# The activations' buffers moved off the weight buffers' place modulo 512 bytes

## The chip, the cores and the metric

The kernel runs on one core of a Trainium2 chip. The metric is the device time of one execution in microseconds (us). A core has a matrix engine (TensorE, PE in the profile; its weight loads are listed as PEld), a vector engine (VectorE, DVE), a scalar engine (ScalarE, ACT), GpSimd (POOL) and a queue that issues DMAs (SyncE, SP). They work side by side and wait for each other through semaphores. On-chip memory (SBUF) has 128 partitions; a tile occupies the same byte range in each of them, so "place" and "distance" below are byte addresses within a partition. Matmul results go to another memory, PSUM.

## The reference

One decoder layer on 256 tokens of width 2048, in float32: a norm, one wide projection `w_in`, three branches that are gated and summed, an output projection, and a squared-ReLU MLP, each with a residual, and a last norm.

```python
proj = rms_norm(x, norm_mix_g) @ w_in                   # 2048 x 11264
u_s5, u_lru, q, k, v, gate_logits = split(proj)
merged = (g_s5 * (s5(u_s5) @ w_br_s5) + g_lru * (rglru(u_lru) @ w_br_lru)
          + g_attn * (stick_breaking(q, k, v) @ w_br_attn))
h = x + merged @ w_out
h = h + square(relu(rms_norm(h, norm_mlp_g) @ w_up)) @ w_down   # hidden width 8192
return rms_norm(h, final_norm_g)
```

The S5 and RG-LRU branches are scans over the tokens, the third is an attention over 8 heads. Inside the S5 branch stands one more weight matrix, `w_glu`.

## The kernel before

All large matrix products run in pieces of one size. A weight **unit** is 256 rows by 512 columns of a weight matrix (two groups of 128 rows); the list `stream` has 520 of them, in the order in which they are used. A unit is loaded by DMA into a `raw` tile (`load_next`, L130) and split into two tiles of a reduced-precision type (`split_next`): ScalarE writes the high part `hi` (L146), VectorE the low part `lo` = raw - hi (L147). The activations are split in the same way into a high and a low part. A product is then the sum of three matmuls, high x high, high x low and low x high.

A matmul has a stationary operand of 128 x 128, which a separate instruction (a weight load, LDWEIGHTS, on PEld) brings into the engine, and a moving operand of 256 or 512 columns that streams past it. The load for the next matmul is issued while the current one streams. There are two kinds of product:

- `chunk` (matmuls at L225 to L227) has the weights stationary and 256 columns of activations moving. It serves `w_in` for the branches' inputs u, k and q, and `w_glu`: 72 units, 24 matmuls each.
- `chunk_tok` (L241 to L243) and `pair_tok` (L276 to L278) have the activations stationary and 512 columns of weights moving. They serve all other units, 12 matmuls each. In the very last chunk eight units do half of their work in pieces of 256 columns.

Smaller matmuls stand in between: those of the S5 scan (`ps_v` at L665 from the tile `stk`, `ps_y` at L653), of attention (`ps_z`, `ps_c`, `ps_o` from `kT`, `tri`, `vt`), of the RG-LRU gates and of the norms. Their work is spread over the stream by generators that `pump` advances after every unit. The order of the matmuls on PE is that of the program.

The tiles come from pools that lie one behind another in SBUF, each tile on a multiple of 32 bytes. The pools up to `tmp` are, in this order:

| pool | tiles | bytes of one | place modulo 512 |
|---|---|---|---|
| `const` | par, ones, tri and others | small | ones, tri: 160 |
| `wraw` | raw x 3 | 4096 | 32 |
| `whi` | hi x 4, lo x 4 | 4096 | 32 |
| `act` | m16 (xT, merged, hT), xhi (xhi, hhi), xlo (xlo, hlo) | 16384 | 32 |
| `ypool` | yhi x 2, ylo x 2 | 8192 | 32 |
| `tmp` | gate x 3, gbias | 2048 | 32 |

The slices of a tile that a matmul reads start at multiples of 512 bytes, so two slices have the distance of their tiles modulo 512. Behind `tmp` lies the pool `s5`, whose small tiles `rad` (128 bytes) and `fw` (256 bytes) bring what follows them to 416 modulo 512: `stk` (which shares its buffer with `wrwi`), the tiles of the RG-LRU branch, and `kT`, `qT`, `vt`, `z` and `s` of attention. These are 384 bytes away from the weight buffers modulo 512, `tri` 128 bytes.

The tags `yhi` and `ylo` hold, one after another, the high and low parts of the RG-LRU branch (`ylru_hi`, `ylru_lo`), two scratch tiles of the S5 scan, the parts of the attention's output, of the gated S5 output and of the merged branches, and the MLP's hidden values (`hd_hi`, `hd_lo`).

Of the kernel before, what the change touches and what calls it, by code (L numbers as in the profile page):

```python
# [9 lines left out]
F32 = mybir.dt.float32  # L10
F32R = mybir.dt.float32r
# [3 lines left out]
P = 128  # L15
L = 256
D = 2048
KT = D // P
# [3 lines left out]
WT = W // P  # L22
NG = 64
NT = 4
# [22 lines left out]
def hybrid_block(ctx: ExitStack, tc: tile.TileContext, io, out):  # L47
# [5 lines left out]
    whi = ctx.enter_context(tc.tile_pool(name="whi", bufs=4))  # L53
    act = ctx.enter_context(tc.tile_pool(name="act", bufs=1))
    ypool = ctx.enter_context(tc.tile_pool(name="ypool", bufs=2))
    tmp = ctx.enter_context(tc.tile_pool(name="tmp", bufs=2))
    psm = ctx.enter_context(tc.tile_pool(name="psm", bufs=4, space=PSUM))
    pss = ctx.enter_context(tc.tile_pool(name="pss", bufs=4, space=PSUM))
# [234 lines left out]

    tc.keep_in_program_order(nc.scalar.preload_act_table_set("natural_log_exp_and_others"))
    gm = small("norm_mix_g")
    xT = act.tile([P, KT, L], F32, tag="m16", name="xT")
    xhi = act.tile([P, KT, L], F32R, tag="xhi", name="xhi")
    xlo = act.tile([P, KT, L], F32R, tag="xlo", name="xlo")
    load_x(0)
    for q in range(3):  # L300
        load_next()
# [212 lines left out]
        yield  # L514
        yield from lru_load()

    ylru_hi = ypool.tile([P, WT, L], F32R, tag="yhi", name="ylru_hi")
    ylru_lo = ypool.tile([P, WT, L], F32R, tag="ylo", name="ylru_lo")

    def lru_half(c, us):  # L520
        parts = []
# [111 lines left out]
    gq = []  # L633

    def s5_scan():
        v = ypool.tile([P, 2, NT, L], F32, tag="yhi", name="s5_v")
        t12 = ypool.tile([P, 2, NT, L], F32, tag="ylo", name="s5_t")
        vr, vi, t1, t2 = v[:, 0], v[:, 1], t12[:, 0], t12[:, 1]
        tabs, more = s5_tables(0)
        yield from more  # L640
        s5_split(0)
        yield
        yield
        for t in range(NT):
            s5_stack(t)
            yield
        tt = nc.vector.tensor_tensor

        def out_products(b):
            ps = pss.tile([P, CH], F32, tag="ps", name=f"ps_y{b}")  # L650
            for k, w_ in enumerate((t2, t1)):
                for t in range(NT):
                    nc.tensor.matmul(ps[t * 32:t * 32 + 32, 0:L], ce[:, k, b * NT + t, :, :], w_[:, t, :], start=k == 0, stop=k == 1,  # L653
                                     skip_group_check=True, tile_position=(0, t * 32))
            nc.vector.scalar_tensor_tensor(us5[:, b, :], us5[:, b, :], dsk[:, b:b + 1], ps[:, 0:L], ALU.mult, ALU.add)
            if b % 2:
                gq.append(later([gelu(b)], 1.0))

        for b in range(WT):
            c, s = tabs  # L660
            t3 = pp.tile([P, NT, L], F32, tag="t3", name=f"t3_{b}")
            for t in range(NT):
                ps = pss.tile([P, CH], F32, tag="ps", name=f"ps_v{b}")
                for i in range(2):
                    nc.tensor.matmul(ps[:, i * L:(i + 1) * L], stk[:, t, 1, i * P:(i + 1) * P], stk[:, t, 0, :], start=i == 0, stop=True,  # L665
                                     skip_group_check=True)
                nc.scalar.copy(v[:, :, t, :], v2(ps))
                if t % 2:
                    yield
            more = iter(())  # L670
            if b + 1 < WT:
                s5_split(b + 1)
                tabs, more = s5_tables(b + 1)
                yield
            next(more, None)
            if b:
                out_products(b - 1)
            yield
            tt(t1, vr, c, ALU.mult)
            yield  # L680
            tt(t2, vi, s, ALU.mult)
            yield
            tt(t1, t1, t2, ALU.add)
            yield
            tt(t3, vi, c, ALU.mult)
            yield
            tt(vr, vr, s, ALU.mult)
            yield
            tt(t3, t3, vr, ALU.subtract)
            next(more, None)  # L690
            yield
            for x_ in (t1, t3):
                for t in range(NT):
                    j = b * NT + t
                    tt_scan(x_[:, t, :], rad[:, j:j + 1].broadcast_to([P, L]), x_[:, t, :])
                    if b + 1 < WT and x_ is t1:
                        s5_stack(t)
                    yield
            next(more, None)
            tt(t2, t1, c, ALU.mult)  # L700
            yield
            tt(vr, t3, s, ALU.mult)
            next(more, None)
            yield
            tt(t2, t2, vr, ALU.subtract)
            yield
            tt(vi, t3, c, ALU.mult)
            yield
            tt(t1, t1, s, ALU.mult)
            yield  # L710
            tt(t1, t1, vi, ALU.add)
            yield
        for _ in range(3):
            yield
        out_products(WT - 1)
# [26 lines left out]
            if n % step == step - 1:  # L742
                yield

    merged = act.tile([P, KT, L], F32, tag="m16", name="merged")
    m_tok = merged.rearrange("p k l -> p (k l)").rearrange("p (t c) -> p t c", t=2)

    def gates(idx, c, alloc):
# [39 lines left out]

    at = ExitStack()
    ap_ = at.enter_context(tc.tile_pool(name="attn", bufs=1))  # L790
    ya_hi = ypool.tile([P, WT, L], F32R, tag="yhi", name="ya_hi")
    ya_lo = ypool.tile([P, WT, L], F32R, tag="ylo", name="ya_lo")
    Z = 384

    def diag(t):
# [84 lines left out]
        finish(t)  # L880


    yg_hi = ypool.tile([P, WT, L], F32R, tag="yhi", name="yg_hi")
    yg_lo = ypool.tile([P, WT, L], F32R, tag="ylo", name="yg_lo")
    for q in range(4):
        s = slice(2 * q, 2 * q + 2)
        nc.scalar.activation(yg_hi[:, s, :], us5[:, s, :], AF.Copy, scale=0.5)
        nc.vector.scalar_tensor_tensor(yg_lo[:, s, :], us5[:, s, :], 0.5, yg_hi[:, s, :].bitcast(F32), ALU.mult, ALU.subtract)
    ys_hi = ypool.tile([P, WT, L], F32R, tag="yhi", name="ys_hi")
    ys_lo = ypool.tile([P, WT, L], F32R, tag="ylo", name="ys_lo")  # L890
    for c in range(2):
        banks = chunk("w_glu", c, W, lambda kt: (yg_hi[:, kt, :], yg_lo[:, kt, :]))
        for j in range(2):
# [10 lines left out]

    def split_pair(i, n, src):
        if mg[i // 8] is None:
            mg[i // 8] = tuple(ypool.tile([P, WT, L], F32R, tag=t, name=f"mg_{t}{i}") for t in ("yhi", "ylo"))
        h_, l_ = mg[i // 8]
        d = slice(i % 8, i % 8 + n)
        nc.scalar.copy(h_[:, d, :], src)  # L910
        nc.vector.tensor_tensor(l_[:, d, :], src, h_[:, d, :].bitcast(F32), ALU.subtract)
# [32 lines left out]

    later([x_load()], 1.0)
    mf.append(chained(mq, split_tok(3, mlp.tile([P, 4, L], F32, tag="reluT", name="mT3", bufs=2))))
    hT = act.tile([P, KT, L], F32, tag="m16", name="hT")
    hhi = act.tile([P, KT, L], F32R, tag="xhi", name="hhi")
    hlo = act.tile([P, KT, L], F32R, tag="xlo", name="hlo")
    h_tok = mlp.tile([P, 2, D], F32, name="h_tok")  # L950

    def ms(kt):
# [114 lines left out]
    for q in range(NQ):  # L1067
        hd, hf = {}, {}

        def up_done(cu, banks):  # L1070
            c = cu % (FQ // CH)
            if c % 2 == 0:
                hd[c // 2] = (ypool.tile([P, WT, L], F32R, tag="yhi", name=f"hd_hi{q}_{c}"),
                              ypool.tile([P, WT, L], F32R, tag="ylo", name=f"hd_lo{q}_{c}"))
            h_, l_ = hd[c // 2]
            r = mlp.tile([P, 2, CH], F32, tag="relu", name=f"relu{q}_{c}", bufs=2)
            for t in range(2):
                nc.scalar.activation(r[:, t, :], banks[t], AF.Relu)
            k = slice((c % 2) * 4, (c % 2) * 4 + 4)
            hf[c] = chained(hq, hidden(r, h_[:, k, :], l_[:, k, :], f"{q}_{c}"))  # L1080

        if q == 0:
            pair_tok("w_up", 0, D, hs, up_done)
        for c in range(0 if q else 2, FQ // CH):
            up_done(c, chunk_tok("w_up", q * (FQ // CH) + c, D, hs))

        def hs_(kt):
            need(hq, hf[kt // 4])
            h_, l_ = hd[kt // 8]
            return h_[:, kt % 8, :], l_[:, kt % 8, :]  # L1090

        for task in tasks:
            finish(task)

        def down_done(c, banks):
            s = slice(c * CH, (c + 1) * CH)
            for t in range(2):
                down_evac(t, s, banks[t])
            if q == NQ - 1:
                for t in range(2):  # L1100
                    square(t, s, c)
                    if c > 0:
# [78 lines left out]
```

## Time and profile before

| | us |
|---|---|
| median of 2 runs | 1491.62 (1490.56 to 1492.67) |
| the profiled execution | 1491.41 |
| its span, first to last instruction | 1489.7 |

The busy time of an engine is the union of its instructions' times. Rows of groups give a line, engine, operation, output <- inputs (tile names without buffer numbers), size and count, then the busy time in us and the mean duration of one in ns. Matmuls are pipelined: a row of 389 ns overlaps with the next one, and the distance between starts is shorter than that. Rows of a stretch give from:to in us, the length, and for each engine the busy time with the number of its instructions that touch the stretch. Rows of the timeline begin with an instruction's start and duration in us.

### The profile page before, as it was taken

What the parts mean: (1) busy time and instruction counts of PE and PEld (TensorE: products, weight loads), DVE (VectorE), ACT (ScalarE), POOL (GpSimd) and SP (SyncE); (2) the same over time, 40 slices, a digit from 0 to 9 for tenths busy, and PEclk for the clock granted to TensorE, in tenths of its full rate; (3) what the DMA queues carried; (4) which work ended last, traced back from release to release, by engine and by line L of the source; (5) the groups of instructions that cost most, each with busy time, mean ns of one, the idle gap of its engine ahead of it and who ended that gap; (6) DMA issues with size and microseconds to landing.
All of it is one profiled execution on the core that took longest, in us unless ns stands there. A gap on an engine that the chain in (4) does not pass through costs nothing.

```text
span 1489.7 us, 19903 instructions
## 1 busy us (share of the span) xinstructions
PE 1478.5 (99%) x7518; PEld 1259.3 (85%) x7518; DVE 1175.7 (79%) x1470; ACT 775.4 (52%) x915; POOL 48.4 (3%) x73
## 2 busy tenths in 40 slices
PE   9999999999999999999999999999999999999997
PEld 9998888989888888888888888888888888888886
DVE  6878999887989998789799896568754886458955
ACT  6767556565765564544454544344433453344443
POOL 1400000000000000000000000000000000000010
PEclk9999999999999999999999999999999999999999
DMA  9557776655556756566856657666666566666664
GB/s 274 189 157 216 209 229 208 184 165 188 170 177 199 224 184 210 188 187 210 268 183 189 195 184 222 189 193 188 200 194 196 187 197 197 192 190 196 189 198 137
DMA packets 89570, 292.41 MB, mean 196 GB/s; under 512 B 12802, under 2 KB 17026, under 8 KB 89346
## 3 DMA queue, kind: packets, MB, share of 16 engines
q1 hardware_dynamic: 89042, 290.55, 62.5%
q8 instruction: 59, 0.97, 0.3%
q10 hardware_dynamic: 432, 0.59, 0.1%
q14 instruction: 37, 0.30, 0.1%
HBM read 282.71 MB, written 2.10 MB: 191 GB/s over the span
## 4 chain that ended last, share of the span: by engine, by line
PE 95%; DVE 2%; ACT 1%; DMA 1%; issue 1%; DVEq 0%; ACTq 0%; SPq 0%
PE mt_w_in L241 7%; PE mt_w_in L243 7%; PE mt_w_in L242 7%; PE mt_w_up L241 7%; PE mt_w_up L243 7%; PE mt_w_up L242 7%; PE mp_w_down L278 4%; PE mp_w_down L277 4%; PE mp_w_down L276 4%; PE mt_w_down L242 4%; PE mt_w_down L241 4%; PE mt_w_down L243 4%; PE mm_w_in L225 3%; PE mm_w_in L227 3%; PE mm_w_in L226 3%; PE mt_w_br_attn L241 1%
## 5 line engine op out<-in xcount | busy, mean ns | idle before, releaser
L146 ACT CAST hi<-raw 128x1024 fp32r<-128x1024 f32 (+1 forms) x521 | 545.2, 1050 | 614.2 <-PE mt_w_up L243 116.8
L147 DVE TENSOR_TENSOR lo<-raw,hi 128x1024 fp32r<-128x1024 f32 (+1 forms) x521 | 637.1, 1224 | 276.2 <-ACT hi L146 268.5
L241 PE MATMUL mt_w_in<-hi,xhi 128*128 128x512 f32 x448 | 176.2, 393 | 0.0
L243 PE MATMUL mt_w_in<-hi,xlo 128*128 128x512 f32 x448 | 174.5, 389 | 0.0
L242 PE MATMUL mt_w_in<-lo,xhi 128*128 128x512 f32 x448 | 174.4, 389 | 0.0
L241 PE MATMUL mt_w_up<-hi,hhi 128*128 128x512 f32 x448 | 174.3, 389 | 0.0
L242 PE MATMUL mt_w_up<-lo,hhi 128*128 128x512 f32 x448 | 174.3, 389 | 0.0
L243 PE MATMUL mt_w_up<-hi,hlo 128*128 128x512 f32 x448 | 174.3, 389 | 0.0
L225 PE MATMUL mm_w_in<-xhi,hi 128*128 128x256 f32 x512 | 146.7, 287 | 0.7 <-ACT hi L146 0.7
L227 PE MATMUL mm_w_in<-xhi,lo 128*128 128x256 f32 x512 | 145.6, 285 | 1.4 <-DVE lo L147 1.4
L226 PE MATMUL mm_w_in<-xlo,hi 128*128 128x256 f32 x512 | 145.6, 285 | 0.0
L741 DVE STREAM_TRANSPOSE reluT<-relu 32x256 f32<-32x256 f32 x256 | 111.5, 436 | 4.2
L242 PE MATMUL mt_w_down<-lo,hd_hi 128*128 128x512 f32 (+1 forms) x272 | 102.5, 377 | 0.0
L241 PE MATMUL mt_w_down<-hi,hd_hi 128*128 128x512 f32 (+1 forms) x272 | 102.4, 377 | 0.0
L243 PE MATMUL mt_w_down<-hi,hd_lo 128*128 128x512 f32 (+1 forms) x272 | 102.4, 376 | 0.0
L225 PEld LDWEIGHTS mm_w_in<-xhi,hi 128*128 128x128 f32 x512 | 99.1, 194 | 1.9 <-ACT hi L146 1.0
L227 PEld LDWEIGHTS mm_w_in<-xhi,lo 128*128 128x128 f32 x512 | 98.8, 193 | 1.9 <-DVE lo L147 1.8
L276 PE MATMUL mp_w_down<-hi,hd_hi 128*128 128x512 f32 x256 | 99.6, 389 | 0.0
L277 PE MATMUL mp_w_down<-lo,hd_hi 128*128 128x512 f32 x256 | 99.6, 389 | 0.0
L278 PE MATMUL mp_w_down<-hi,hd_lo 128*128 128x512 f32 x256 | 99.6, 389 | 0.0
L226 PEld LDWEIGHTS mm_w_in<-xlo,hi 128*128 128x128 f32 x512 | 99.2, 194 | 0.1
L243 PEld LDWEIGHTS mt_w_in<-hi,xlo 128*128 128x128 f32 x448 | 84.1, 188 | 17.7
(294 smaller groups left out, 2358.1 us busy)
## 6 DMA issues: line engine op xcount, KB each, us to landing
raw<-in_w_in SPq DMA_DIRECT2D x175, 512.0 KB, 4.2
raw<-in_w_up SPq DMA_DIRECT2D x128, 512.0 KB, 4.3
raw<-in_w_down SPq DMA_DIRECT2D x128, 512.0 KB, 4.2
raw<-in_w_out SPq DMA_DIRECT2D x32, 512.0 KB, 4.4
raw<-in_w_br_lru SPq DMA_DIRECT2D x16, 512.0 KB, 4.6
raw<-in_w_br_attn SPq DMA_DIRECT2D x16, 512.0 KB, 4.3
raw<-in_w_br_s SPq DMA_DIRECT2D x16, 512.0 KB, 4.3
stk<-ux SPq DMA_DIRECT2D x96, 64.0 KB, 4.3
```

Of the source, the lines that this page charges most:

```text
L146: anchor["act"] = nc.scalar.copy(h[:, k, :], r[:, k, :]).ins
L147: anchor["dve"] = nc.vector.tensor_tensor(l_[:, k, :], r[:, k, :], h[:, k, :].bitcast(F32), ALU.subtract).ins
L225: nc.tensor.matmul(o, wh[:, kk, s], xh, start=first and ct % 2 == 0, stop=False, skip_group_check=True)
L226: nc.tensor.matmul(o, wh[:, kk, s], xl, start=False, stop=False, skip_group_check=True)
L227: mm = nc.tensor.matmul(o, wl[:, kk, s], xh, start=False, stop=last and ct % 2 == 1, skip_group_check=True)
L241: nc.tensor.matmul(banks[j], xh[:, s], wh[:, a:b], start=kt == 0, stop=False)
L242: nc.tensor.matmul(banks[j], xh[:, s], wl[:, a:b], start=False, stop=False)
L243: return nc.tensor.matmul(banks[j], xl[:, s], wh[:, a:b], start=False, stop=kt == ng * UK - 1)
L276: nc.tensor.matmul(o, xh[:, s], wh[:, kk, :], start=kt == 0, stop=False)
L277: nc.tensor.matmul(o, xh[:, s], wl[:, kk, :], start=False, stop=False)
L278: mm = nc.tensor.matmul(o, xl[:, s], wh[:, kk, :], start=False, stop=kt == ng * UK - 1)
L741: nc.vector.transpose(d_[32 * a:32 * a + 32, :, :, 32 * b:32 * b + 32], s_[32 * b:32 * b + 32, :, :, 32 * a:32 * a + 32])
```

## The change

Every tile of the activations' high and low parts, and the tiles that share their tags, get a few unused floats at their end: 8 behind m16, 16 behind xhi, 8 behind xlo, and 24 behind each of the two yhi and two ylo buffers. A helper makes the wider tile and gives out a view of its first columns in the old shape.

```diff
+    def ytile(shape, dt, tag, name, pool=None, pad=24):
+        n = math.prod(shape[1:])
+        t = (pool or ypool).tile([P, n + pad], dt, tag=tag, name=name)[:, 0:n]
+        k = " ".join(f"d{i}" for i in range(len(shape) - 1))
+        return t.rearrange(f"p ({k}) -> p {k}", **{f"d{i}": d for i, d in enumerate(shape[1:])})
...
-    xT = act.tile([P, KT, L], F32, tag="m16", name="xT")
-    xhi = act.tile([P, KT, L], F32R, tag="xhi", name="xhi")
-    xlo = act.tile([P, KT, L], F32R, tag="xlo", name="xlo")
+    xT = ytile([P, KT, L], F32, "m16", "xT", act, 8)
+    xhi = ytile([P, KT, L], F32R, "xhi", "xhi", act, 16)
+    xlo = ytile([P, KT, L], F32R, "xlo", "xlo", act, 8)
...
-    ylru_hi = ypool.tile([P, WT, L], F32R, tag="yhi", name="ylru_hi")
-    ylru_lo = ypool.tile([P, WT, L], F32R, tag="ylo", name="ylru_lo")
+    ylru_hi = ytile([P, WT, L], F32R, tag="yhi", name="ylru_hi")
+    ylru_lo = ytile([P, WT, L], F32R, tag="ylo", name="ylru_lo")
```

The same replacement is made for every other tile of these tags (`merged`, `hT`, `hhi`, `hlo`, `s5_v`, `s5_t`, `ya_*`, `yg_*`, `ys_*`, `mg_*`, `hd_*`). The places that result, as distances from the weight buffers modulo 512, are: m16 0, xhi 32, xlo 96, the two yhi buffers 128 and 224, the two ylo buffers 320 and 416. The pads sum to 512 bytes, so that `tmp` and everything behind it keeps its place modulo 512. In the list above, `act` and `ypool` are all that moves.

More of the change, by code (lines that the diff above doesn't have):

```diff
@@ L635, in s5_scan @@
     def s5_scan():
-        v = ypool.tile([P, 2, NT, L], F32, tag="yhi", name="s5_v")
-        t12 = ypool.tile([P, 2, NT, L], F32, tag="ylo", name="s5_t")
+        v = ytile([P, 2, NT, L], F32, tag="yhi", name="s5_v")
+        t12 = ytile([P, 2, NT, L], F32, tag="ylo", name="s5_t")
         vr, vi, t1, t2 = v[:, 0], v[:, 1], t12[:, 0], t12[:, 1]
@@ L743, in blocks @@
                 yield
-    merged = act.tile([P, KT, L], F32, tag="m16", name="merged")
+    merged = ytile([P, KT, L], F32, "m16", "merged", act, 8)
     m_tok = merged.rearrange("p k l -> p (k l)").rearrange("p (t c) -> p t c", t=2)
@@ L790, in hybrid_block @@
     ap_ = at.enter_context(tc.tile_pool(name="attn", bufs=1))
-    ya_hi = ypool.tile([P, WT, L], F32R, tag="yhi", name="ya_hi")
-    ya_lo = ypool.tile([P, WT, L], F32R, tag="ylo", name="ya_lo")
+    ya_hi = ytile([P, WT, L], F32R, tag="yhi", name="ya_hi")
+    ya_lo = ytile([P, WT, L], F32R, tag="ylo", name="ya_lo")
     Z = 384
@@ L880, in hybrid_block @@
         finish(t)
-    yg_hi = ypool.tile([P, WT, L], F32R, tag="yhi", name="yg_hi")
-    yg_lo = ypool.tile([P, WT, L], F32R, tag="ylo", name="yg_lo")
+    yg_hi = ytile([P, WT, L], F32R, tag="yhi", name="yg_hi")
+    yg_lo = ytile([P, WT, L], F32R, tag="ylo", name="yg_lo")
     for q in range(4):
@@ L888, in hybrid_block @@
         nc.vector.scalar_tensor_tensor(yg_lo[:, s, :], us5[:, s, :], 0.5, yg_hi[:, s, :].bitcast(F32), ALU.mult, ALU.subtract)
-    ys_hi = ypool.tile([P, WT, L], F32R, tag="yhi", name="ys_hi")
-    ys_lo = ypool.tile([P, WT, L], F32R, tag="ylo", name="ys_lo")
+    ys_hi = ytile([P, WT, L], F32R, tag="yhi", name="ys_hi")
+    ys_lo = ytile([P, WT, L], F32R, tag="ylo", name="ys_lo")
     for c in range(2):
@@ L906, in split_pair @@
         if mg[i // 8] is None:
-            mg[i // 8] = tuple(ypool.tile([P, WT, L], F32R, tag=t, name=f"mg_{t}{i}") for t in ("yhi", "ylo"))
+            mg[i // 8] = tuple(ytile([P, WT, L], F32R, tag=t, name=f"mg_{t}{i}") for t in ("yhi", "ylo"))
         h_, l_ = mg[i // 8]
@@ L946, in hybrid_block @@
     mf.append(chained(mq, split_tok(3, mlp.tile([P, 4, L], F32, tag="reluT", name="mT3", bufs=2))))
-    hT = act.tile([P, KT, L], F32, tag="m16", name="hT")
-    hhi = act.tile([P, KT, L], F32R, tag="xhi", name="hhi")
-    hlo = act.tile([P, KT, L], F32R, tag="xlo", name="hlo")
+    hT = ytile([P, KT, L], F32, "m16", "hT", act, 8)
+    hhi = ytile([P, KT, L], F32R, "xhi", "hhi", act, 16)
+    hlo = ytile([P, KT, L], F32R, "xlo", "hlo", act, 8)
     h_tok = mlp.tile([P, 2, D], F32, name="h_tok")
@@ L1072, in up_done @@
             if c % 2 == 0:
-                hd[c // 2] = (ypool.tile([P, WT, L], F32R, tag="yhi", name=f"hd_hi{q}_{c}"),
-                              ypool.tile([P, WT, L], F32R, tag="ylo", name=f"hd_lo{q}_{c}"))
+                hd[c // 2] = (ytile([P, WT, L], F32R, tag="yhi", name=f"hd_hi{q}_{c}"),
+                              ytile([P, WT, L], F32R, tag="ylo", name=f"hd_lo{q}_{c}"))
             h_, l_ = hd[c // 2]
```

## The prediction

> **What bounds the kernel now.** I read the page's busy times and chain of waits first, then the instruction groups by shape, then the busy time of chosen stretches, and last the timeline of single matmuls and weight loads.
>
> ```profile
> span 1489.7 us, 19903 instructions
> PE 1478.5 (99%) x7518; PEld 1259.3 (85%) x7518; DVE 1175.7 (79%) x1470; ACT 775.4 (52%) x915; POOL 48.4 (3%) x73
> PEclk9999999999999999999999999999999999999999
> PE 95%; DVE 2%; ACT 1%; DMA 1%; issue 1%; DVEq 0%; ACTq 0%; SPq 0%
> ```
>
> PE is busy 99% of the span, at the full granted clock, and carries 95% of the chain that ends last. So the kernel's time is the number of matmuls times the distance from one matmul's start to the next, plus some 5% of waits. The change adds and removes no instruction. It can only act through that distance, or through the durations on the engines that PE waits for.
>
> The distance can be read from how many matmuls touch a stretch in which PE does nothing else.
>
> ```profile
> core 0: us, PE busy (x), PEclk, DMA share, GB/s
> 20.00:40.00 20.00, 20.00 (x169) 1.00 0.95 274
> 1000.00:1200.00 200.00, 200.00 (x884) 1.00 0.61 194
> ...
> L241 PE MATMUL mt_w_up<-hi,hhi 128*128 128x512 f32 x448 | 174.3, 389 | 0.0
> L225 PE MATMUL mm_w_in<-xhi,hi 128*128 128x256 f32 x512 | 146.7, 287 | 0.7 <-ACT hi L146 0.7
> ```
>
> From 1000 to 1200 us run only 128x512 matmuls (w_up, w_down). Each row lasts 389 ns because matmuls overlap, so the ones that touch the stretch number (200 + 0.389) / distance: 200.389 / 884 = 226.7 ns. From 20 to 40 us run only 128x256 ones (w_in): (20 + 0.287) / 169 = 120.0 ns. The 256 columns between them cost 106.7 ns, or 0.417 ns each. So 512 columns need 213.4 ns and 256 need 106.7, and **both kinds of matmul carry the same 13.3 ns that no column explains**. That remainder is what moving buffers can change.
>
> How many pay it follows from the weight units:
>
> ```profile
> L146 ACT CAST hi<-raw 128x1024 fp32r<-128x1024 f32 (+1 forms) x521 | 545.2, 1050 | 614.2 <-PE mt_w_up L243 116.8
> ```
>
> There are 520 units (the first is split in two pieces). 72 of them go through chunk with 24 matmuls of 256 columns, 448 through chunk_tok and pair_tok with 12 of 512; the eight units of the last chunk have six of 512 and twelve of 256 each. That makes 72 x 24 + 8 x 12 = 1824 matmuls of 256 and 448 x 12 - 8 x 6 = 5328 of 512: 7152 in all, and 7152 x 13.3 ns = 95 us.
>
> **The change, part by part.** (1) The helper takes a wider tile and a view of its first columns: no instruction, nothing to pay. (2) No engine's order, queue or DMA changes. The pads are 32, 64, 32 and four times 96 bytes, 512 in sum, so tmp and all pools behind it keep their places modulo 512, and raw, hi, lo, stk, kT, vt and tri do as well. (3) VectorE and ScalarE read and write the activations' parts at new distances. VectorE's rows show two distances already, 384 bytes (lru_tc or lru_xc with ylru_hi) and 0 (the glu tile with ys_hi), in the same operation and size:
>
> ```profile
> L570 DVE TENSOR_TENSOR ylru_lo<-lru_xc,ylru_hi 128x512 fp32r<-128x512 f32 x2 | 1.4, 688 | 0.4 <-ACT ylru_hi L569 0.4
> L570 DVE TENSOR_TENSOR ylru_lo<-lru_tc,ylru_hi 128x512 fp32r<-128x512 f32 x2 | 1.4, 679 | 0.0
> L901 DVE TENSOR_TENSOR ys_lo<-glu,ys_hi 128x512 fp32r<-128x512 f32 x4 | 2.6, 683 | 0.0
> ```
>
> 688 and 679 around 683 ns: I take nothing, bounded by 5 ns on each, and beside PE's work at that. (4) On PE a matmul that streams weights (or activations) now runs over the load of a stationary tile 32, 96, 128, 224, 320 or 416 bytes away modulo 512, in place of 0. The rest of this part prices that.
>
> When do the two reads overlap at all? The load for the next matmul starts with the current one, and two loads in a row start 0.11 us apart (the second row: two loads of 0.19 each, 0.30 together):
>
> ```profile
> 1000.03 0.19 PEld L242 LDWEIGHTS mt_w_up<-lo,hhi 128*128 128x128 f32 x1
> 138.10 0.30 PEld L665 LDWEIGHTS ps_v<-stk 96*128 96x128 f32 x2 [0.47 <-DMA stk<-ux]
> ...
> 1000.02 0.39 PE L241 MATMUL mt_w_up<-hi,hhi 128*128 128x512 f32 x1
> ```
>
> So a load of 128 columns (512 bytes) takes about 0.11 us, in which the stream passes 256 columns (1024 bytes): half of a 512-wide matmul, the whole of a 256-wide one. The same 13.3 ns in both kinds fits a cost that each load puts on the stream, and it fits just as well a fixed cost of each new stationary tile. **Why I expect the distance not to matter:** the stream moves twice as fast as the load, so during one load their distance runs through all 512 bytes once wherever it begins. A different start moves the moment at which they meet in one bank; it doesn't take the meeting away.
>
> The trace tests this in a few places, since stk, kT and vt lie 384 and tri 128 bytes away from hi, lo and the activations even now. First a load of stk under a 256-wide matmul (the row with the 362.96 start), and the matmuls before it at distance 0:
>
> ```profile
> 362.73 0.28 PE L225 MATMUL mm_w_in<-xhi,hi 128*128 128x256 f32 x1
> 362.85 0.28 PE L226 MATMUL mm_w_in<-xlo,hi 128*128 128x256 f32 x1
> 362.96 0.28 PE L227 MATMUL mm_w_in<-xhi,lo 128*128 128x256 f32 x1
> L227 PE MATMUL mm_w_in<-xhi,lo 128*128 128x256 f32 x2 | 0.6, 283 | 0.0
> L226 PE MATMUL mm_w_in<-xlo,hi 128*128 128x256 f32 x1 | 0.3, 283 | 0.0
> ```
>
> 283 ns with 384 bytes between them, as with 0: nothing is gained. Then loads of tri (128 bytes), kT (384) and stk (384) under 512-wide matmuls, with a neighbour at distance 0:
>
> ```profile
> L243 PE MATMUL mt_w_in<-hi,xlo 128*128 128x512 f32 x1 | 0.4, 396 | 0.0
> L242 PE MATMUL mt_w_in<-lo,xhi 128*128 128x512 f32 x1 | 0.4, 389 | 0.0
> ...
> L243 PE MATMUL mt_w_br_lru<-hi,ylru_lo 128*128 128x512 f32 x1 | 0.4, 396 | 0.0
> ```
>
> Each is 396 ns against 389, so 7 ns slower, not faster (309.95, 378.87 and 134.23 us into the span are the neighbours' starts). But that can be the disturbance alone. At 131.93 us a load at distance 0 starts late, and the matmuls from there on are 396, 396 and 397 ns, with no odd distance anywhere:
>
> ```profile
> 131.93 0.40 PE L241 MATMUL mt_w_br_lru<-hi,ylru_hi 128*128 128x512 f32 x1
> 131.99 0.19 PEld L242 LDWEIGHTS mt_w_br_lru<-lo,ylru_hi 128*128 128x128 f32 x1
> L241 PE MATMUL mt_w_br_lru<-hi,ylru_hi 128*128 128x512 f32 x1 | 0.4, 396 | 0.0
> L242 PE MATMUL mt_w_br_lru<-lo,ylru_hi 128*128 128x512 f32 x1 | 0.4, 396 | 0.0
> L243 PE MATMUL mt_w_br_lru<-hi,ylru_lo 128*128 128x512 f32 x1 | 0.4, 397 | 0.0
> 133.33 0.39 PE L241 MATMUL mt_w_br_lru<-hi,ylru_hi 128*128 128x512 f32 x1
> ```
>
> By 133.33 us it is back at 0.39. So the pair of streams has a rhythm that it falls back into after a disturbance. A distance that is constant is no disturbance that recurs, and I expect the same rhythm at 226.7 and 120.0 ns. The bounds of the unknown cost of a distance, per matmul: +7 ns on each 512-wide one and 0 on a 256-wide one (the rows above), and -13.3 ns on each (the whole remainder). I take 0, the value of the 256-wide rows, which are the nearest case: there the distance changed and the rhythm didn't. The 7 ns I put down to the disturbance.
>
> The Trainium skill states on SBUF — State Buffer, section Who interferes with whom, that PE has two independent read ports, one for the moving operand and one for weight loads, and never waits on another engine. By that rule the change does nothing; the 283 ns rows agree, and the 396 ns rows at least don't contradict it.
>
> **The sum.** 0 + 0 + 0 + 7152 x 0 = 0 against the profiled execution's own time, 1491.4 us (1489.7 of span and 1.7 around it). The median of the two runs shown is 1491.6, so it needs no correction.
>
> **The rivals.** Slower: each constant distance keeps the streams out of the good rhythm, as every one of the loads at 128 and 384 bytes does for its one matmul. Then 5328 x 7 ns = 37 us are added: 1528.7 us, +2.5%. Against it stands that the late load at distance 0 shows the same 396 ns, and that 256-wide matmuls show nothing. It passes 2% (29.8 us) from 5.6 ns per matmul on; were it true of only some of the six distances, it would stay below.
>
> Faster: the 13.3 ns are collisions of the two reads that need equal places modulo 512, and the new distances avoid them. All of it gives 1491.4 - 95 = 1396 us; half, if some distances still collide, 1444 us. It decides from a third of the remainder on (29.8 of 95 us). VectorE would allow it: its busiest stretch fills 91%, and PE's work there would shrink by 13.3 / 226.7, or 6%.
>
> ```profile
> 200.00:300.00 100.00, 100.00 (x641) 90.49 (x640) 91.08 (x97) 57.34 (x63) 4.98 (x4) 1.00 0.68 202
> ```
>
> For it speaks that the remainder is the same for both widths, as a cost per load would be. Against it speak that a load 384 bytes away removed none of the remainder, and the two speeds. What the trace cannot exclude is a bank pattern that repeats every 128 bytes: 384 and 128 would then look like 0, and 32, 96, 224, 320 and 416 would not.
>
> The Trainium skill has a rule that makes this rival larger than zero: TensorE: Matmul & The Clock Gate, section Back-to-back issue gap, gives N / 2.4 + 2.5 ns for a warm matmul, so 215.8 and 109.2 ns. If the distances brought matmuls there, 10.9 x 5328 + 10.8 x 1824 ns = 78 us would go, an estimate from that page, and the time would be 1414 us; this trace's 226.7 and 120.0 ns don't show such gaps.
>
> **How the numbers follow.** No effect (1491.4 us, its own range 1487 to 1496 from settling after some other number of disturbances, each worth a few times 7 ns): 0.64. Slower by the lost rhythm, up to 1528.7: 0.16, of which 0.04 stays within 2%. Faster, 1396 to 1480: 0.20, of which 0.02 stays within 2%. That is faster 0.18, same 0.70, slower 0.12, with 2% as about what a measurement of this kernel can tell from no change. The range takes the first two cases, 0.80: from 1487 to 1529 us.
>
> **What would show it.** Right: some 884 matmuls touch 200 us of pure w_up and w_down, the 512-wide rows stay at 389 ns and the 256-wide ones at 283, and no new group appears in the waits. The slower rival: 396 ns as the mean of mt_w_up, and about 858 matmuls in 200 us. The faster rival: durations below 389, and more than 884, first in one tile's rows (hhi at 32, hlo at 96, hd_hi at 128 or 224), which would tell which distance matters. My sum is wrong in kind if PE shows idle time that it has not now, which would mean that the views of padded tiles changed what waits for what.

## The result and the profile after

| | us |
|---|---|
| before, median of 2 runs | 1491.62 |
| after, median of 2 runs | 1513.22 (1512.94 to 1513.51) |
| after / before | 1.0145, 95% interval 1.0101 to 1.0188 |
| span of the profiled execution, before and after | 1489.7, 1511.8 |

The change costs 22 us. From the page of the kernel after: the span, the busy time, the granted clock, the chain, and the groups of instructions that answer to those of before (busy us, mean ns of one):

```profile
span 1511.8 us, 19903 instructions
PE 1497.7 (99%) x7518; PEld 1254.6 (83%) x7518; DVE 1176.4 (78%) x1470; ACT 773.9 (51%) x915; POOL 47.5 (3%) x73
PEclk9999999999999999999999999999999999999999
PE 93%; DVE 2%; DMA 2%; ACT 1%; issue 1%; SPq 0%; DVEq 0%; ACTq 0%
...
L247 PE MATMUL mt_w_up<-hi,hhi 128*128 128x512 f32 x448 | 177.9, 397 | 0.0
...
L248 PE MATMUL mt_w_up<-lo,hhi 128*128 128x512 f32 x448 | 176.1, 393 | 0.0
L249 PE MATMUL mt_w_up<-hi,hlo 128*128 128x512 f32 x448 | 174.3, 389 | 0.0
...
L231 PE MATMUL mm_w_in<-xhi,hi 128*128 128x256 f32 x512 | 144.7, 283 | 0.5 <-ACT hi L152 0.5
```

The instructions are the same in number, the clock is still full, VectorE and ScalarE are within 1.5 us of before. PE alone is busy longer, by 1497.7 - 1478.5 = 19.2 us; its idle time (span less busy) goes from 11.2 to 14.1 us. The code lines have moved by six: L247 to L249 are L241 to L243 of before.

Next the PE columns of three stretches, first before (the row that was not shown yet), then after:

```profile
0.00:100.00 100.00, 96.87 (x747) 1.00 0.69 215
```

```profile
core 0: us, PE busy (x), PEclk, DMA share, GB/s
0.00:100.00 100.00, 93.96 (x740) 1.00 0.68 212
20.00:40.00 20.00, 20.00 (x172) 1.00 0.94 256
1000.00:1200.00 200.00, 200.00 (x867) 1.00 0.60 190
```

By the prediction's way of reading, 512-wide matmuls now stand (200 + 0.39) / 867 = 231.1 ns apart (before 226.7), and 256-wide ones (20 + 0.28) / 172 = 117.9 ns (before 120.0). So **the 512-wide ones became 4.4 ns slower and the 256-wide ones 2 ns faster**. 5328 x 4.4 - 1824 x 2.1 = 23.4 - 3.8 = 19.6 us, about the 19.2 us of added busy time. The faster ones bring little: they stand mostly near the start, where PE also waits for weights, and the first 100 us hold 93.96 us of PE work in place of 96.87. That is the 2.9 us of added idle time. A new wait stands there too, 1.2 us of `ps_n` for xT; as the kernel with moved weights below shows it with 1.1 us, without any padded activation tile, it comes from the faster matmuls and not from the views.

The timeline of after, from 999.82 us on, shows the rhythm (start, duration):

```profile
999.82 0.39 PE L249 MATMUL mt_w_up<-hi,hlo 128*128 128x512 f32 x1
1000.05 0.40 PE L247 MATMUL mt_w_up<-hi,hhi 128*128 128x512 f32 x1
1000.28 0.39 PE L248 MATMUL mt_w_up<-lo,hhi 128*128 128x512 f32 x1
1000.52 0.39 PE L249 MATMUL mt_w_up<-hi,hlo 128*128 128x512 f32 x1
...
1001.90 0.39 PE L249 MATMUL mt_w_up<-hi,hlo 128*128 128x512 f32 x1
```

From the first row to the last are nine distances in 2.08 us, 231.1 ns each. A matmul's duration tells its own distance: 389 ns goes with 226.7 before, a difference of 162, so 397, 393 and 389 mean 235, 231 and 227 ns. The full-precision starts give 235.0, 231.7 and 226.7, again and again. Their sum is three times 226.67 plus 13.3: **in every three matmuls 13.3 ns are added, twice 6.67, which is the time of 16 columns** (16 x 0.417 ns). Summed by stage from start to start in both traces, waits included, w_in's wide part gives +6.6 us, w_up +6.5, w_down +6.3, w_out +1.7, the branches +2.0 together, and the two 256-wide stages -0.4 (w_in, where the waits eat the gain) and -0.2 (w_glu).

### The profile page after: what moved, and what is told of

The parts are those of the page before. It is cut to its first block, busy times and chain, and to the rows that moved or that the text cites. A ratio compares the mean times of both kernels' runs of the same rounds, so it can differ in the third digit from the quotient of the medians.

```text
span 1511.8 us, 19903 instructions
## 1 busy us (share of the span) xinstructions
PE 1497.7 (99%) x7518; PEld 1254.6 (83%) x7518; DVE 1176.4 (78%) x1470; ACT 773.9 (51%) x915; POOL 47.5 (3%) x73
## 4 chain that ended last, share of the span: by engine, by line
PE 93%; DVE 2%; DMA 2%; ACT 1%; issue 1%; SPq 0%; DVEq 0%; ACTq 0%
PE mt_w_up L247 7%; PE mt_w_in L247 7%; PE mt_w_in L248 7%; PE mt_w_in L249 7%; PE mt_w_up L248 7%; PE mt_w_up L249 7%; PE mp_w_down L283 4%; PE mp_w_down L282 4%; PE mp_w_down L284 4%; PE mt_w_down L248 4%; PE mt_w_down L247 4%; PE mt_w_down L249 4%; PE mm_w_in L233 2%; PE mm_w_in L232 2%; PE mm_w_in L231 2%; DMA raw<-in_w_in 2%
## 5 line engine op out<-in xcount | busy, mean ns | idle before, releaser
L247 PE MATMUL mt_w_in<-hi,xhi 128*128 128x512 f32 x448 | 178.5, 398 | 0.0
L247 PE MATMUL mt_w_up<-hi,hhi 128*128 128x512 f32 x448 | 177.9, 397 | 0.0
L249 PE MATMUL mt_w_in<-hi,xlo 128*128 128x512 f32 x448 | 176.3, 393 | 0.0
L249 PE MATMUL mt_w_up<-hi,hlo 128*128 128x512 f32 x448 | 174.3, 389 | 0.0
L247 PE MATMUL mt_w_down<-hi,hd_hi 128*128 128x512 f32 (+1 forms) x272 | 103.2, 380 | 0.0
L249 PE MATMUL mt_w_down<-hi,hd_lo 128*128 128x512 f32 (+1 forms) x272 | 103.0, 379 | 0.0
L249 PEld LDWEIGHTS mt_w_up<-hi,hlo 128*128 128x128 f32 x448 | 84.1, 188 | 20.8
L249 PEld LDWEIGHTS mt_w_in<-hi,xlo 128*128 128x128 f32 x448 | 84.0, 188 | 20.1
L247 PEld LDWEIGHTS mt_w_up<-hi,hhi 128*128 128x128 f32 x448 | 84.1, 188 | 19.7
L247 PEld LDWEIGHTS mt_w_in<-hi,xhi 128*128 128x128 f32 x448 | 84.1, 188 | 19.6 <-issue 0.8
```

Source lines behind the costliest of these rows:

```text
L247: nc.tensor.matmul(banks[j], xh[:, s], wh[:, a:b], start=kt == 0, stop=False)
L249: return nc.tensor.matmul(banks[j], xl[:, s], wh[:, a:b], start=False, stop=kt == ng * UK - 1)
```

## The experiments

Four theories are named in the expectations. **A, alternation**: a constant distance is free; the change costs because the distance differs from one load to the next (hhi, hhi, hlo at 32, 32, 96). **B**: any distance other than 0 costs by itself. **C**: each distance has a price of its own. **D**, formed after the first four runs: the two reads meet in a pattern of 256 bytes; a 512-wide matmul has two stalls of 6.67 ns at 0 modulo 256 and up to three elsewhere. A ratio stands where a kernel was timed several times beside the kernel before; a single time is one execution. Runs of before beside them had medians from 1489.99 to 1490.22 us, and distances follow from the counts and durations as above, or (where tenths are given) from the starts in the trace. Rows carry the line numbers of their own kernel.

### One distance for everything: 32 and 256 bytes

```diff
-    def ytile(shape, dt, tag, name, pool=None, pad=24):
+    def ytile(shape, dt, tag, name, pool=None, pad=0):
...
     xT = ytile([P, KT, L], F32, "m16", "xT", act, 8)
-    xhi = ytile([P, KT, L], F32R, "xhi", "xhi", act, 16)
-    xlo = ytile([P, KT, L], F32R, "xlo", "xlo", act, 8)
+    xhi = ytile([P, KT, L], F32R, "xhi", "xhi", act, 0)
+    xlo = ytile([P, KT, L], F32R, "xlo", "xlo", act, 0)
...
```

This is against the changed kernel, and hhi and hlo are made like xhi and xlo; the second kernel has 64 in place of the 8 behind xT (and behind merged and hT, which share its buffer). The buffers of yhi and ylo get no pad in either, so that all the activations' parts lie 32 (or 256) bytes from the weights; tmp and the pools behind it move along.

> All activation parts lie at one and the same distance, 32 bytes, from the weight buffers. Theory A (alternation: the stationary tiles of one triple lie at two different distances, and each switch disturbs the rhythm): the 512-wide matmuls are back at 226.7 ns from start to start and 389 ns in the rows, and the time is 1492 us, plus or minus 5. Theory B (a distance other than 0 costs by itself): the 512-wide matmuls stay at 229 to 235 ns and the time is 1505 to 1520 us. Theory C (a distance has its own cost, of either sign): neither value is fixed; a mean below 226.7 ns would show that 0 is not the best place.

> All activation parts lie 256 bytes from the weight buffers modulo 512. Theory D (the two reads meet in a memory pattern of 256 bytes; at a distance of 0 modulo 256 a load costs the 512-wide stream two stalls of 6.67 ns, elsewhere up to three): the 512-wide matmuls stand at 226.7 ns from start to start, the 256-wide ones at 120.0, and the time is 1490 us, plus or minus 4. Theory B (any distance other than 0 costs): 512-wide matmuls at 233.3 ns as with 32 bytes, and 1520 us.

Measured: 32 bytes 1521.64 us, ratio 1.0211 (1.0194 to 1.0228); 256 bytes 1490.63 us, ratio 1.0001 (0.9991 to 1.0010). Groups and stretches, first of the kernel with 32 bytes:

```profile
L247 PE MATMUL mt_w_up<-hi,hhi 128*128 128x512 f32 x448 | 177.3, 396 | 0.0
L248 PE MATMUL mt_w_up<-lo,hhi 128*128 128x512 f32 x448 | 177.3, 396 | 0.0
L249 PE MATMUL mt_w_up<-hi,hlo 128*128 128x512 f32 x448 | 177.3, 396 | 0.0
```

```profile
20.00:40.00 20.00, 20.00 (x172) 1.00 0.92 256
1000.00:1200.00 200.00, 200.00 (x859) 1.00 0.59 187
```

and of the kernel with 256 bytes:

```profile
L247 PE MATMUL mt_w_up<-hi,hhi 128*128 128x512 f32 x448 | 174.4, 389 | 0.0
```

```profile
20.00:40.00 20.00, 20.00 (x169) 1.00 0.94 253
1000.00:1200.00 200.00, 200.00 (x884) 1.00 0.62 193
```

With 32 bytes there is no alternation left, and every 512-wide matmul takes 200.396 / 859 = 233.3 ns, more than in the changed kernel: A falls. (396 ns and about 858 matmuls in 200 us are what the prediction named as the sign of its slower rival.) With 256 bytes nothing differs from before, 884 and 169 to the last matmul: B falls, and the repeat after 256 bytes that D says is there.

### Which distance costs what

One helper for four kernels gives each tile a buffer 512 bytes larger and starts its view at a listed offset. A smaller buffer for DMA descriptors makes the room. The offsets shown are those of the first kernel.

```diff
+OFF = {'hd_hi0_0': 32, 'hd_lo0_0': 32, 'hd_hi0_2': 64, 'hd_lo0_2': 64, ...}
+    def ytile(shape, dt, tag, name, pool=None, pad=0):
+        n = math.prod(shape[1:])
+        o = OFF.get(name, 0) // 4
+        t = (pool or ypool).tile([P, n + 128], dt, tag=tag, name=name)[:, o:o + n]
```

> High and low part of each activation lie at the same distance, but each pair at another one: hd pairs 32 to 256 bytes in steps of 32, RG-LRU output 288, attention 320, S5 output 352, merged 384 and 416, hhi and hlo 448, xhi and xlo 480. Theory A: every stage of 512-wide matmuls shows 389 ns in its rows. Theory B: every stage shows 392 to 398 ns. Theory C: the stages differ from each other by more than 3 ns, some perhaps below 389.

> The high parts lie at distance 0 as before the change, each low part at another distance: 32 to 256 for the hd tiles, then 288 (RG-LRU), 320 (attention), 352 (S5), 384 and 416 (merged), 448 (hlo), 480 (xlo). Theory A: all stages are slower than 389 ns, by about the 4 ns per matmul of the change. Theory B: only the matmuls that run over the load of a low part (one in three) are slower, so the mean over a triple rises by a third of what equal distances cost. Theory C: differs from stage to stage.

> High and low part at the same distance, in steps of 4 bytes: hd pairs 4, 8, 12, 16, 20, 24, 28 and 48 bytes, RG-LRU 40, attention 56, S5 80, merged 112 and 144, hhi and hlo 272, xhi and xlo 16. Theory A: 389 ns everywhere. Theory B: 392 to 398 ns everywhere, unless it is a step of 16 or 32 bytes that counts. Theory C: a pattern by the distance modulo 16, 32 or 64 bytes, which would tell the grain of the memory.

> High and low part at the same distance, places just below 0 and around 256: hd pairs 508, 504, 500, 496, 488, 472, 464 and 36 bytes, RG-LRU 252, attention 260, S5 248, merged 264 and 240, hhi and hlo 244, xhi and xlo 256. Theory D: what a place costs repeats after 256 bytes (260 as 4: 232; 264 as 8: 231; 504 as 248; 500 as 244; 496 as 240), and no place is below 226.7 ns, since fewer than two stalls do not occur for 512 columns. Rival: some place next to 0 has fewer stalls, at 220 ns, and would make a kernel faster than the one before the change.

Single times: 1513.29, 1512.52, 1515.69 and 1510.51 us. Mean distances from start to start of the 512-wide matmuls in ns, by the distance of their stationary tile in bytes, worked out from the starts (matmuls within six of a wait or another kind are left out):

```
high and low parts alike
  multiples of 32   32:233.2  64:233.4  96:234.2 128:232.4 160:233.3 192:228.9 224:233.1 256:227.0
                   288:233.1 320:233.2 352:234.1 384:232.9 416:233.3 448:228.9 480:233.3
  finer              4:232.3   8:230.6  12:230.0  16:233.3  20:233.3  24:231.1  28:228.6
                    40:233.4  48:233.3  56:233.3  80:232.1 112:233.3 144:233.3 272:233.3
  near 256 and 512 240:228.4 244:233.3 248:233.3 252:228.7 260:232.4 264:230.7
                   464:232.0 472:232.3 488:231.1 496:228.3 500:233.3 504:233.3 508:228.3
high parts at 0, low parts at the distance
                    32:233.2  64:231.2  96:232.4 128:231.4 160:233.1 192:231.3 224:230.9 256:227.1
                   288:233.2 320:231.1 352:232.5 384:231.2 416:233.3 448:231.1 480:231.2
```

The kernel with w_in's activations at 256 and the MLP's at 464 bytes shows both prices among its groups:

```profile
L250 PE MATMUL mt_w_in<-lo,xhi 128*128 128x512 f32 x448 | 174.7, 390 | 0.0
L249 PE MATMUL mt_w_up<-hi,hhi 128*128 128x512 f32 x448 | 176.6, 394 | 0.0
```

Most distances stand at 233.3 ns, 226.67 and one more stall of 6.67; none is better than 0 or 256, and 192 and 448 are the next best of the multiples of 32, at 228.9. A mix of 0 for two loads and another distance for the third costs 4.2 to 6.6 ns on the mean of three, so one badly placed load in three is enough for most of the cost. The repeat after 256 bytes that D says holds at the near places too (4 and 260, 8 and 264, 244 and 500, 248 and 504); its limit of three stalls doesn't quite (234.2 ns at 96).

Three of these means hide two values. At 252 bytes the RG-LRU matmuls stand near 233.3 ns up to 141 us and at 226.7 from 165 to 240 us; 28 and 508 bytes change between the same two values from one block of matmuls to the next. The w_in matmuls at 16 bytes, not in the table, stand at 233.3 ns for most of the stage and at 226.7 in the last 192, from 624 us on.

### The two halves of the change

The first kernel keeps the distances of xhi and xlo (32, 96) and puts the yhi and ylo buffers at 0; the second keeps 128, 224, 320 and 416 and puts xhi and xlo at 0. The diff is the first one's against the changed kernel (hlo is made like xlo); the second has pads of 0, 0 and 32 behind xT, xhi and xlo and keeps the 24.

```diff
-    def ytile(shape, dt, tag, name, pool=None, pad=24):
+    def ytile(shape, dt, tag, name, pool=None, pad=0):
...
-    xlo = ytile([P, KT, L], F32R, "xlo", "xlo", act, 8)
+    xlo = ytile([P, KT, L], F32R, "xlo", "xlo", act, 104)
```

> Part of the change alone: xhi and xlo (and hhi, hlo in their buffers) at 32 and 96 bytes, the y buffers at 0. If each stage pays by its own distance, this takes half of the loss: 1319 matmuls over xhi and xlo x 5.0 ns, 1535 over hhi and hlo x 4.2 ns, less some 2 us in the 256-wide ones: 1490 + 11 = 1501 us. If the loss came from one buffer or from a crowded memory as a whole, it would be 1490 or 1512.

> The other part alone: the yhi and ylo buffers at 128, 224, 320 and 416 bytes, xhi and xlo at 0. By its own distances: 2,400 matmuls over y tiles x 4.2 ns: 1490 + 10 = 1500 us, and only_act and only_y together give the whole change's 21 us. In w_in and w_up 389 ns, in w_down 392 to 394 ns.

Measured: 1505.37 us and 1499.62, so +15.2 and +9.4 beside 1490.19 of before; their sum, 24.6, is near the whole change's 21.6 (single executions, 3 us apart); 1501 and 1500 us had been expected, so the first half costs 4 us more than expected. Groups of the first, then of the second:

```profile
L248 PE MATMUL mt_w_up<-lo,hhi 128*128 128x512 f32 x448 | 176.8, 395 | 0.0
L282 PE MATMUL mp_w_down<-hi,hd_hi 128*128 128x512 f32 x256 | 99.7, 390 | 0.0
```

```profile
L248 PE MATMUL mt_w_up<-lo,hhi 128*128 128x512 f32 x448 | 174.4, 389 | 0.0
L283 PE MATMUL mp_w_down<-lo,hd_hi 128*128 128x512 f32 x256 | 100.8, 394 | 0.0
```

The cost sits where the distance is, and only there. It was not the same in size, though: w_up with 32 and 96 bytes stood at 232.1 ns here and at 231.1 in the whole change, with the same distances. The starts show both values inside each kernel: here w_up goes at 231.1 ns for some 220 matmuls (from 827 to 876 us) and at 232.2 for the rest, and in the whole change w_in goes at 232.2 ns and only at its end at 231.2. So three loads at 32, 32 and 96 bytes have two paces, and a stage can change from one to the other.

### Matmuls alone, without other engines

Kernel before, with 2880 matmuls (not 3360, as the expectation counts) added at its end whose results nobody reads. The moving tile `mv` is hhi, the stationary one `st_` is hlo; only the start of the stationary slice shifts.

```diff
+    def bench(kind, n, m, dists, reps):
+        for i, d in enumerate(dists):
+            ps = pss.tile([P, CH], F32, tag="ps", name=f"{kind}_{chr(97 + i // 8)}{chr(97 + i % 8)}")
+            for _ in range(reps):
+                nc.tensor.matmul(ps[0:m, 0:n], st_[:, d // 4:d // 4 + m], mv[:, 0:n], start=True, stop=True, skip_group_check=True)
+
+    bench("wide", 512, 128, range(0, 512, 16), 30)
+    bench("half", 256, 128, range(0, 512, 16), 30)
+    bench("thin", 512, 64, range(0, 512, 32), 30)
+    bench("fine", 512, 128, range(0, 64, 4), 30)
```

> The kernel before, with 3360 matmuls more at its end that nothing reads, when all other engines are idle: hhi moving, hlo stationary, each group of 30 at one distance. Groups: 512 columns moving with a stationary tile of 128 columns, at 0 to 496 bytes in steps of 16; the same with 256 columns moving; 512 moving with a stationary tile of 64 columns, in steps of 32; and 512 with 128 at 0 to 60 bytes in steps of 4. Theory D (the reads of a load and of the stream meet, and the cost comes from these meetings): 226.7 ns from start to start at 0 and 256 and up to 233.3 elsewhere, as in the kernel, and half as many stalls for a load of half the size, so about 220 ns (213.3 + 6.7) with 64 columns. If the 13.3 ns were a fixed cost of each new stationary tile, the load of 64 columns would stay at 226.7. If other engines' reads took part, the groups would be at 226.7 whatever the distance.

The span is 2040.6 us with them. Groups of this kernel by shape; the last letter counts steps of 16 bytes, the one before it steps of 128 (thin: 32 and 256), so wide_aa is 0, wide_ac 32, wide_ca 256, half_ae 64, half_bg 224:

```profile
L1122 PE MATMUL wide_aa<-hhi,hlo 128*128 128x512 f32 x30 | 7.0, 390 | 0.0
L1122 PE MATMUL wide_ac<-hhi,hlo 128*128 128x512 f32 x30 | 7.2, 395 | 0.0
L1122 PE MATMUL wide_ba<-hhi,hlo 128*128 128x512 f32 x30 | 7.2, 395 | 0.0
L1122 PE MATMUL wide_ca<-hhi,hlo 128*128 128x512 f32 x30 | 7.0, 389 | 0.0
L1122 PE MATMUL wide_cc<-hhi,hlo 128*128 128x512 f32 x30 | 7.2, 395 | 0.0
...
L1122 PE MATMUL half_aa<-hhi,hlo 128*128 128x256 f32 x30 | 3.8, 283 | 0.0
L1122 PE MATMUL half_ae<-hhi,hlo 128*128 128x256 f32 x30 | 3.6, 276 | 0.0
L1122 PE MATMUL half_bg<-hhi,hlo 128*128 128x256 f32 x30 | 3.7, 279 | 0.0
...
L1122 PE MATMUL thin_aa<-hhi,hlo 128*64 128x512 f32 x30 | 7.1, 392 | 0.0
L1122 PE MATMUL thin_ac<-hhi,hlo 128*64 128x512 f32 x30 | 7.1, 395 | 0.0
```

The other engines ended their work at 1485.4 us, 3 us after the first of these matmuls. A stretch among the 512-wide ones (PE, PEld, DVE, ACT and POOL, then clock, DMA share and GB/s):

```profile
1500.00:1600.00 100.00, 100.00 (x434) 81.06 (x433) 0.00 (x0) 0.00 (x0) 0.00 (x0) 1.00 0.00 0
```

With VectorE, ScalarE and DMA out of play the cost is the same: 0 gives 226.7 ns, 32 and 128 bytes 233.4, and from 256 bytes on the values repeat those from 0 on. So no other engine's work is needed for it: it lies in PE's own reads. Nor is it the buffer in PSUM: the results go to four buffers in turn, so 0, 64, 128 and 192 bytes write to the same one and differ. That it is the distance of the two that counts, and not the stationary tile's place by itself, is shown for 256 columns: 116.7 ns stand here at 480 bytes, in most of w_in when the weights are moved on by 480 bytes (below), and in most of w_in when the moving activations are moved on by 32 and the weights stay (the kernel with 32 bytes above). For 512 columns every run moved the stationary tile alone. **For 256 columns the best place is another one**: 120.0 ns at 0, 116.7 at 224, 113.3 at 64, where only 6.67 ns stand beside the columns. The thin rows refute a price per loaded column: a load of half as many columns leaves 226.6 to 232.5 ns, where half the stalls would give 220. So D has the period and the size of a stall right, but a collision for each column read is not what makes it.

At 0 the rhythm is found again after the switch to it: the distances of wide_aa begin 234, 236, 228, 232, 231, 227 and then stay at 226.7.

### Does the rhythm depend on what went before?

Same added code, 1440 matmuls: twelve blocks of 40 (`one` is the inner loop of `bench` for a single place) in the order 0, 16, 32, 16, 0, 240, 32, 240, 64, 16, 0, 16 bytes (past_a to past_l), and blocks of 384 and 128 columns and with loads of 32 columns.

```diff
...
+    for i, d in enumerate((0, 16, 32, 16, 0, 240, 32, 240, 64, 16, 0, 16)):
+        one(f"past_{chr(97 + i)}", 512, 128, d)
+    bench("three", 384, 128, range(0, 256, 32), 40)
+    bench("quarter", 128, 128, range(0, 256, 32), 40)
+    bench("slim", 512, 32, range(0, 256, 32), 40)
```

> The kernel before with other matmuls at its end, 40 of a kind, hhi moving and hlo stationary. First 512 columns at the distances 0, 16, 32, 16, 0, 240, 32, 240, 64, 16, 0, 16 in this order: if a place alone sets the cost, all groups at 16 agree (and those at 240); if the rhythm depends on what went before, 16 is at 226.7 ns behind 0 and at 233.3 behind 32 or 64. Then 384 and 128 columns moving, and 512 columns over a load of only 32 columns, each at 0 to 224 bytes in steps of 32. If each column that is loaded takes its share of the 13.3 ns, a load of 32 columns leaves about 217 ns; if any load costs the same two or three stalls, 226.7 to 233.3.

Groups of this kernel:

```profile
L1127 PE MATMUL past_b<-hhi,hlo 128*128 128x512 f32 x40 | 9.2, 389 | 0.0
L1127 PE MATMUL past_d<-hhi,hlo 128*128 128x512 f32 x40 | 9.5, 395 | 0.0
L1127 PE MATMUL past_f<-hhi,hlo 128*128 128x512 f32 x40 | 9.2, 389 | 0.0
L1127 PE MATMUL past_h<-hhi,hlo 128*128 128x512 f32 x40 | 9.3, 390 | 0.0
L1127 PE MATMUL past_l<-hhi,hlo 128*128 128x512 f32 x40 | 9.2, 389 | 0.0
...
L1122 PE MATMUL quarter_aa<-hhi,hlo 128*128 128x128 f32 x40 | 4.6, 273 | 0.0
...
L1122 PE MATMUL slim_aa<-hhi,hlo 128*32 128x512 f32 x40 | 9.4, 394 | 0.0
```

Sixteen bytes cost nothing after 0 (b and l, 389 ns) and a full stall after 32 (d, 395 ns, 233.3 apart, for all 40 matmuls). So one place has two rhythms that hold themselves, and here the block before decides which one is entered; the two values at 16, 28, 252 and 508 bytes and in w_up above are of the same kind. 240 bytes gives 226.7 after 0 (f) and 228.3 after 32 (h). 0 itself always finds back. With 384 columns the distances of the starts lie from 173.3 to 176.8 ns; 128 columns stand at 111.6 at every place, where the loads follow each other without a gap (PEld is never idle there), and with loads of 32 columns the 512-wide matmuls stand at 230.4 to 239.9 ns, slower than with full loads at some places (231.8 against 226.7 at 0) and faster at others (230.9 against 233.4 at 128).

### Taking the gain and leaving the loss

The two kinds of matmul want different places, so the activations stay where they were, and only the weight tiles of the units that go through chunk (72 of 520) get a view that starts 480 or 64 bytes further on. The diff against the kernel before is that of 480 bytes (120 floats); the other has 16 in its place, and both have the smaller descriptor buffer of the kernels above. The sign of the distance turns, as weights are the stationary operand there: 480 further on is the place of a chunk under the 32 bytes above.

```diff
-        h = whi.tile([P, UK, CH], F32R, tag="hi", name=f"hi{i}")
-        l_ = whi.tile([P, UK, CH], F32R, tag="lo", name=f"lo{i}")
+        o = 120 if stream[i][0] == "w_glu" or (stream[i][0] == "w_in" and stream[i][1] < 8) else 0
+        h, l_ = (whi.tile([P, UK * CH + 128], F32R, tag=n_, name=f"{n_}{i}")[:, o:o + UK * CH].rearrange("p (k c) -> p k c", k=UK)
+                 for n_ in ("hi", "lo"))
```

> The kernel before, with the weight tiles of the 256-wide matmuls alone (w_in for u, k and q, and w_glu) read and written 480 bytes further, so that their distance is that of the change's better side, and all 512-wide ones at 0. The descriptors' scratch is halved to make room. Theory D: the 256-wide matmuls stand at 117 ns in place of 120, the 512-wide ones stay at 226.7; of 1728 matmuls the 768 of u wait for their weights anyhow, so 960 x 3.1 ns = 3 us are gained: 1487 us, -0.2%. Rival: ScalarE and VectorE set the pace there too, and nothing is gained: 1490 us.

> As chunk_only, but the weight tiles of the 256-wide matmuls lie 64 bytes further in place of 480. The separate measurement showed 113.3 ns for 256 columns at 64 bytes, the lowest of all places, and 116.7 at 480. If a place costs the same in the kernel as alone: the 256-wide matmuls stand at 113.3 ns, 960 of them gain 6.7 ns or 6 us, and the time is 1484 us if nothing waits in their stead, 1486.5 if half of it is lost to waits as with 480 bytes. Rival: alternating high and low parts break the rhythm, and it is no better than 480: 1488 us.

Measured: 480 bytes 1488.34 us, ratio 0.9988 (0.9979 to 0.9997); 64 bytes 1486.70 us, ratio 0.9976 (0.9965 to 0.9986). **The second beats both kernels**, before by 3.5 us or 0.24%. Its busy times, its stretches, its groups, and what PE waited for (us in total, times, longest):

```profile
PE 1470.1 (99%) x7518; PEld 1249.6 (84%) x7518; DVE 1175.2 (79%) x1470; ACT 774.8 (52%) x915; POOL 49.3 (3%) x73
```

```profile
0.00:100.00 100.00, 93.99 (x752) 1.00 0.70 217
20.00:40.00 20.00, 20.00 (x178) 1.00 0.95 265
260.00:285.00 25.00, 25.00 (x215) 1.00 0.70 210
330.00:355.00 25.00, 25.00 (x223) 1.00 0.54 169
1000.00:1200.00 200.00, 200.00 (x884) 1.00 0.61 193
```

```profile
L227 PE MATMUL mm_w_glu<-yg_lo,hi 128*128 128x256 f32 x64 | 17.7, 276 | 0.0
L242 PE MATMUL mt_w_up<-hi,hhi 128*128 128x512 f32 x448 | 174.3, 389 | 0.0
```

```profile
PE mm_w_in L228 <- DVE lo L148: 2.7, 3, 1.8
```

The 256-wide matmuls are at 20.28 / 178 = 113.9 ns from 20 to 40 us and at 25.28 / 223 = 113.3 from 330 to 355, the 512-wide ones where they were. But **the gain doesn't hold throughout**: from 260 to 285 us it is 25.28 / 215 = 117.6 ns, and the starts show two rhythms at the same place, 113.3 ns up to 55 us and from 325 us on, 117.8 from 57 to 290 us, which is half of w_in's 256-wide matmuls. The changes of pace come where other matmuls or a wait interrupt them. At 480 bytes w_in stands at 116.7 nearly throughout, as had been expected (117), and the gain is 1.7 of the 3 us expected. PE's busy time falls by 1478.5 - 1470.1 = 8.4 us, but its idle time grows from 11.2 to 1484.8 - 1470.1 = 14.7 us: part of the gain is given back at once. It is given back in the first 100 us, with 93.99 us of PE work in place of 96.87; matmuls that run faster than the weights arrive only wait longer for them (DMA share 0.95 from 20 to 40 us, as before; PE waits 2.7 us for lo, before 1.4, VectorE for hi, and ScalarE waited 21.2 us of these 100 for raw weights, 21.1 before).

## Why the prediction was wrong

The prediction said no change, 1491.4 us; it is 1513.22, 21.8 us more. Its range, to 1529, held the time because it took in the slower rival, not because the sum allowed for it.

- **What bounds the kernel** was right: the time followed the distance between matmuls, and the counts 5328 and 1824 with the measured 4.4 and -2.1 ns give back PE's added busy time. That helper, queues, VectorE and ScalarE bring nothing was right as well (instructions as before, engines within 1.5 us).
- **The step that failed** is the pricing of the distance: "A different start moves the moment at which they meet in one bank; it doesn't take the meeting away", and from it "A distance that is constant is no disturbance that recurs, and I expect the same rhythm at 226.7 and 120.0 ns". The kernel with a constant 32 bytes has no alternation at all and stays at 233.3 ns in every 512-wide matmul; the added matmuls alone do too. The start is just what counts: how many stalls of 6.67 ns fall into a matmul depends on it, from two (226.7 ns at 0) to three (233.3 at 32) in the mean. Whether what it moves is a meeting in a bank, no run tells.
- **The row that misled** was the return to 0.39 us after the late load at 131.93. It showed that *distance 0* finds back to its good rhythm, which the settling of wide_aa confirms. I carried that over to distances at which nothing in the trace showed a settled rhythm, and put their price at nothing. The 396 ns rows at 128 and 384 bytes, which I put down to the disturbance, have the size of the price: 7 ns against 6.67.
- **The nearest case was chosen wrongly.** I took 0 from 256-wide rows with 384 bytes. 256-wide matmuls do react to the distance (113.3 to 120.3 ns), and 384 is 128 modulo 256, where the added ones stand at 120.0 as at 0. The three rows could not show it, and they said nothing of the 512-wide ones, which hold three quarters of the work.
- **The slower rival** had mechanism, place and price, 37 us at most. The change paid 23 us of it because not every matmul gets the extra stall at its distances (in w_up two of three). A constant 32 bytes pays nearly all, at the 396 ns that this rival named and with 859 matmuls in 200 us for its 858: 5328 x 6.67 = 35.5 us, less the 256-wide gain, against a measured 1521.64 - 1490.09 = 31.6.
- **The faster rival** guessed a bank pattern shorter than 512 bytes. There is a period, of 256 and not 128, but place 0, where the kernel stood, is already the best for 512 columns. Only the 256-wide matmuls had something to gain: 1728 x 6.67 = 11.5 us with the weights 64 bytes on. PE's busy time fell by 8.4 of them, as half of w_in fell into the slower rhythm, and 3.5 of the 8.4 went into waits.
- The Trainium skill's rule (SBUF — State Buffer, section Who interferes with whom: two independent read ports, PE never waits on anyone) does not hold in that strength here: with all other engines idle, the place of the stationary slice alone moves a matmul from 226.7 to 233.4 ns.

Shown: the cost follows the place of PE's stationary tile against the moving one, comes in steps of 16 columns, repeats every 256 bytes, and is there without alternation and without other engines. For 512 columns the moving tile itself was never moved, so that there the distance is told from the stationary tile's own place only by analogy with 256 columns. **Not settled** is what a stall is. That fewer loaded columns do not lessen it speaks against a collision for each column read, and that a place has two rhythms speaks for a phase between load and stream that locks in; no run tells what locks, nor why an interruption sometimes leads into the other rhythm.

## What to carry to other kernels

For a stream of matmuls with a fresh weight load each, the place of the stationary tile against the moving one modulo 256 bytes is worth some 3% of a 512-wide float32r matmul and up to 6% of a 256-wide one in these runs, and the best place is a different one for each width (0 and 64 bytes in these runs), so move tiles by view and width and not all at once. Read the effect from how many matmuls touch a fixed stretch, and try one constant distance in a row of added matmuls before reasoning about banks. That a rhythm recovers after a disturbance at one place says nothing about another place: look at the starts over a whole stage, as a mean can hide two rhythms.

## What had not been expected of the hardware

- Of the 13.3 ns that neither width explains, a 256-wide matmul can lose half: 113.3 ns at 64 bytes, against 120.0 at 0. A 512-wide one went below 226.6 at no place that was tried.
- The rhythm has a memory: 16 bytes stand at 226.7 ns after 0 and at 233.3 after 32, through 40 matmuls. It shows in whole kernels too: at 64 bytes w_in's 256-wide matmuls run at 113.3 ns, then at 117.8 for 230 us, then at 113.3 again.
- Loads of a quarter of the columns, whose rows last 109 ns in place of 188, leave the 512-wide matmul at 230.4 to 239.9 ns: slower than a full load at 0, 32 and 192 bytes, 1.5 to 4 ns faster than one at 64, 96 and 128, and never as fast as a full load at 0.
